# Third and fourth state-space tile begun at slots 9 and 14 instead of 8 and 12

## The chip, the cores and the metric

One core of a Trainium2 chip runs the whole layer in one launch. The metric is the device time of that launch in microseconds. The kernel before takes 855.93 us, the median of three runs (855.25 to 856.22).

## The reference, cut to what matters

One layer of a hybrid decoder on 512 tokens of width 1024, in float32. After an RMS norm, one projection gives the inputs of three branches and three gates; the branches are merged under the gates.

```
u, cb, cc, cx, q, k, v, gates = split_columns(rms_norm(x) @ w_in)
y_ssm  = s5_ssm(u, ...)            # 32 groups x 16 channels, 64 complex states per group
y_conv = short_conv(cb, cc, cx)
y_attn = swa_attention(q, k, v)
merged = sum_r sigmoid(gate_r) * (branch_r @ w_branch[r])
x += merged @ w_out;  x += SwiGLU(rms_norm(x));  x += sigmoid(rms_norm(x) @ w_pg) * (p @ w_pp)
```

Inside `s5_ssm` a diagonal complex recurrence runs over time; then `y = Re(C s) + D u`, a gelu, and a gate `y * sigmoid(y @ w_glu)`. Only the place of this state-space work in the program is touched here.

## The kernel before, in words

Every float32 product is made of three matmuls on parts (high and low of weights and of data). So the inner loop of a projection (`gemm_T`, lines 328 to 333) goes by groups of three 512-wide matmuls, and after each group `pump` (line 305) may add one piece of other work. A projection of 128 columns of `w_in` (`z_tile`, line 746) is eight groups; a pair of columns of `w_branch` (`branch`, line 1191) is two times four groups. Weights come by SyncE's DMA queue (`raw`, line 230), are cast to the high part on ScalarE (`hi`, line 245), and the low part is made on VectorE (`lo`, line 246). In this region a half of weights is cast three halves ahead of its use, and the slab after it is loaded when a slab's first half is cast.

The program order of each engine is written out by hand (the tile framework is in its manual mode). Three devices set it:

- `later(d, fn)` emits `fn` at the d-th group from now.
- `peq` holds TensorE work; `pump` emits one entry of it after a group.
- `slot()` (line 1175) is called after each eight groups; it moves every active state-space generator one stage on.

The state-space work is in four tiles of 128 channels (called tile 0 to tile 3), each a generator `ssm_gen` (line 1003), begun at the slot that `SSM_SLOTS` (line 1173) names. Its stages, one a slot:

- stage 0: loads of `tb` and `uu` (lines 1007, 1011).
- stage 1: `E` (1026 and 1028 on VectorE, `ewt` 1027 on GpSimd).
- stage 2: `W` (1067 to 1069) and the load of the tables `cs` (1071); TensorE gets `e_all`, the transposes of E (1039) and small products (1047). ScalarE copies them to `ET` (1040) and `ko` (1053), and SyncE spreads `ko` over `dbuf` (1057).
- stage 3: TensorE gets `v_two` (1083), which reads `ET`. In its own group it emits the first rotation and two groups on the second: `vsw` (1095, 1096 on ScalarE), `mt` and `G` (1092, 1098 on VectorE; `G` reads `cs`), three groups later subtraction, scan and `sv` (1102, 1104, 1111) with `gsw` (1107, 1108 on ScalarE, 1112 on GpSimd), and four groups later the addition 1114.
- stage 5: `Dg` (1123), two copies on ScalarE.
- stage 6: TensorE gets `y_one` (1130, 1132), which reads `Dg`, `sv` and `W`. Its result is copied to `ys` (1137), stored to `sy` (1140), `un` is loaded (1144).
- stage 7: load of `yr` (1150), behind the stores.
- stage 9: the gelu: `yc` (1155, VectorE), `qq` (1157, GpSimd), two VectorE operations two groups later (1163, 1164), the sigmoid on ScalarE four groups later (1167), `yu` (1168), and at seven groups its cast to `yh` on ScalarE (283).

Slots 0 to 4 lie beside the conv branch's merge, 5 to 12 beside the conv gates (each pair followed by two multiplications, 1211), 13 to 24 beside the attention gates and merge: two `z_tile` and one `branch` in turn (slots 15, 18, 21 and 24 come after a `branch`, whose two halves each emit 1200 and 1201 on VectorE). After slot 26 the program needs all four tiles. Each gate's result leaves PSUM by a sigmoid on ScalarE (1186), emitted just ahead of the slot.

Within one step the generators run in the order in which they began. Two lines of stage 9 and one of stage 5:

```
later(4, lambda: act.activation(out=qq, in_=qq, func=AF.Sigmoid, scale=1.5957691216057308))
later(7, lambda: split_ap(yu, ybox[0][0][:, ct], ybox[0][1][:, ct]))
act.copy(out=Dg[r, :, r].rearrange("p a (i q) -> p a i q", q=16), ...)
```

Of the kernel before, what the change touches and what calls it, by code (L numbers as in the profile page):

```python
# [77 lines left out]
def hybrid_trunk_kernel(  # L78
# [1091 lines left out]
        yield  # L1170

    slot_n = [0]
    SSM_SLOTS = {0: 0, 4: 1, 8: 2, 12: 3}

    def slot():
        if slot_n[0] in SSM_SLOTS:
            bg.append(ssm_gen(SSM_SLOTS[slot_n[0]]))
        slot_n[0] += 1
        step()
# [316 lines left out]
```

## Time and profile before

| what | value |
|---|---|
| median of three runs | 855.93 us |
| the profiled execution, its own time | 852.8 us |
| its span, first to last instruction | 851.0 us |
| TensorE busy | 98% of the span, mean granted clock 0.997 |
| VectorE, ScalarE, GpSimd busy | 66%, 45%, 15% |
| state-space tiles, lines 1007 to 1168 | from 175.1 to about 320 us |

The profile is one execution. A timeline's row is an instruction (or several alike, x4) with its start from the span's start, its duration, and in brackets the idle time of its engine before it with what ended it. Names such as `z<-h,hi` are the program's.

### The profile page before, as it was taken

The page shows a single profiled execution, that of the slowest core. Times are in us where ns is not written, and L with a number is a line of the kernel's source. Part 1 is how long each engine was busy: PE and PEld are TensorE (multiplying, and loading weights), DVE is VectorE, ACT ScalarE, POOL GpSimd, SP SyncE. Part 2 cuts the span into 40 slices and gives each one's busy share as a digit, 9 for nine tenths or more (in the row PEclk, how much of TensorE's full clock was granted, in tenths as well). Part 3 has the DMA queues.
Part 4 walks back from the last instruction along what each step waited for, and adds up shares of the span by engine and source line. Part 5 has one row for each costly group of instructions (what it writes and reads, how often), then busy time and mean ns, then how long its engine had stood idle before and what let it go on. Part 6 is the DMA issues. An engine that isn't in the chain of part 4 may idle for free.

```text
span 851.0 us, 10673 instructions
## 1 busy us (share of the span) xinstructions
PE 835.6 (98%) x4053; PEld 693.4 (81%) x4053; DVE 558.3 (66%) x833; ACT 382.9 (45%) x603; POOL 129.7 (15%) x135
## 2 busy tenths in 40 slices
PE   9999999999999999999999999999999999999996
PEld 7988777887877888888889888788888888888885
DVE  4889697848788863676885547644447444457964
ACT  6665657546444532443454333433333233334733
POOL 2040081724233311000003011000000000000201
PEclk9999999999999999999999999999999999999998
DMA  8759567553436359624858989962247422226112
GB/s 316 238 202 331 196 128 196 124 174 128 161 102 204 107 182 251 174 75 149 338 194 259 238 222 293 361 181 95 96 159 241 154 99 99 91 92 216 61 50 99
DMA packets 96035, 150.52 MB, mean 177 GB/s; under 512 B 6937, under 2 KB 67505, under 8 KB 93809
## 3 DMA queue, kind: packets, MB, share of 16 engines
q1 hardware_dynamic: 85056, 117.68, 40.6%
q0 software_dynamic: 10240, 31.46, 16.0%
q10 hardware_dynamic: 688, 0.70, 0.2%
q8 instruction: 32, 0.52, 0.2%
q14 instruction: 19, 0.15, 0.1%
HBM read 138.09 MB, written 43.00 MB: 213 GB/s over the span
## 4 chain that ended last, share of the span: by engine, by line
issue 38%; PE 32%; DVE 12%; DMA 8%; ACT 5%; POOL 5%; POOLq 0%; ACTq 0%; DVEq 0%
PE z L287 7%; PE z L288 7%; PE z L289 7%; DMA T<-T 4%; DMA T<-in_w_ffn_out_dram 2%; DVE lo L246 2%; PE z L1276 1%; PE z L1277 1%; PE z L1275 1%; PE z L1305 1%; PE z L1303 1%; PE z L1304 1%; PE z L683 1%; DVE s_t L853 1%; ACT s_t L867 1%
## 5 line engine op out<-in xcount | busy, mean ns | idle before, releaser
L287 PE MATMUL z<-h,hi 128*128 128x512 f32 (+1 forms) x776 | 293.6, 378 | 0.0
L288 PE MATMUL z<-l,hi 128*128 128x512 f32 (+1 forms) x776 | 290.5, 374 | 0.2 <-DVE l L284 0.2
L289 PE MATMUL z<-h,lo 128*128 128x512 f32 (+1 forms) x776 | 290.3, 374 | 0.0
L246 DVE TENSOR_TENSOR lo<-raw,hi 128x1024 fp32r<-128x1024 f32 (+1 forms) x168 | 206.3, 1232 | 108.4 <-ACT hi L245 107.9
L245 ACT CAST hi<-raw 128x1024 fp32r<-128x1024 f32 (+1 forms) x168 | 171.9, 1031 | 130.6 <-PE z L1305 37.7
L287 PEld LDWEIGHTS z<-h,hi 128*128 128x128 f32 x776 | 146.2, 188 | 26.1 <-issue 1.2
L289 PEld LDWEIGHTS z<-h,lo 128*128 128x128 f32 x776 | 146.1, 188 | 26.1
L288 PEld LDWEIGHTS z<-l,hi 128*128 128x128 f32 x776 | 146.2, 188 | 25.5 <-DVE l L284 0.7
L1303 PE MATMUL z<-hi,fh 128*128 128x512 f32 x180 | 70.8, 393 | 0.0
L1305 PE MATMUL z<-hi,fl 128*128 128x512 f32 x180 | 70.3, 390 | 0.0
L1304 PE MATMUL z<-lo,fh 128*128 128x512 f32 x180 | 70.1, 389 | 0.0
L1390 DVE TENSOR_TENSOR g<-z,g 128x512 f32<-128x512 f32 x22 | 15.2, 692 | 62.0 <-PE z L289 62.0
L1332 POOL TENSOR_SCALAR ms<-ss 128x1 f32<-128x1 f32 x8 | 3.0, 378 | 339.6 <-ACT xn L1329 339.5
L287 PE MATMUL z<-yh,hi 128*128 128x512 f32 x112 | 44.0, 393 | 0.0
L288 PE MATMUL z<-yl,hi 128*128 128x512 f32 x112 | 43.7, 390 | 0.2 <-DVE yl L284 0.2
L289 PE MATMUL z<-yh,lo 128*128 128x512 f32 x112 | 43.6, 390 | 0.0
L1305 PEld LDWEIGHTS z<-hi,fl 128*128 128x128 f32 x180 | 33.8, 188 | 7.5 <-DVE fl L284 0.5
L1304 PEld LDWEIGHTS z<-lo,fh 128*128 128x128 f32 x180 | 33.8, 188 | 6.8
L1303 PEld LDWEIGHTS z<-hi,fh 128*128 128x128 f32 x180 | 33.8, 188 | 6.7
L1382 ACT ACTIVATE g<-z 128x512 f32<-128x512 f32 x22 | 13.2, 598 | 55.2 <-PE z L289 55.2
L283 ACT CAST fh<-g 128x512 fp32r<-128x512 f32 (+1 forms) x22 | 11.2, 511 | 53.0 <-DVE g L1390 53.0
L1310 DVE TENSOR_TENSOR xr<-z,xr 128x512 f32<-128x512 f32 x36 | 24.5, 685 | 8.6 <-PE z L1305 7.9
(274 smaller groups left out, 1092.4 us busy)
## 6 DMA issues: line engine op xcount, KB each, us to landing
raw<-in_w_in_dram SPq DMA_DIRECT2D x23, 1024.0 KB, 5.3
raw<-in_w_ffn_in_dram SPq DMA_DIRECT2D x22, 1024.0 KB, 5.0
raw<-T SPq DMA_DIRECT2D x12, 1024.0 KB, 4.8
T<-in_w_ffn_out_dram POOLq DMA_DIRECT2D x12, 1024.0 KB, 12.0
T<-in_w_out_dram POOLq DMA_DIRECT2D x6, 1024.0 KB, 9.3
raw<-in_w_branch_dram SPq DMA_DIRECT2D x12, 512.0 KB, 3.9
raw<-in_w_ffn_out_dram SPq DMA_DIRECT2D x6, 1024.0 KB, 5.1
T<-in_w_ffn_out_dram POOLq DMA_DIRECT2D x6, 768.0 KB, 8.1
```

Source lines behind the costliest of these rows:

```text
L245: act.copy(out=hi, in_=src)
L246: todo = [lambda: dve.tensor_tensor(lo, src, hi.bitcast(F32), ALU.subtract)]
L283: act.copy(out=hi, in_=src)
L287: pe.matmul(ps, wh, ah, start=first, stop=False)
L288: pe.matmul(ps, wh, al, start=False, stop=False)
L289: pe.matmul(ps, wl, ah, start=False, stop=last)
L1303: pe.matmul(ps, fh[:, f, kk, ts], hi[:, k], start=st, stop=False, skip_group_check=True)
L1304: pe.matmul(ps, fh[:, f, kk, ts], lo[:, k], start=False, stop=False, skip_group_check=True)
L1305: pe.matmul(ps, fl[:, f, kk, ts], hi[:, k], start=False, stop=last, skip_group_check=True)
L1310: dve.tensor_tensor(dst, ps if sign > 0 else dst, dst if sign > 0 else ps, ALU.add if sign > 0 else ALU.subtract)
L1382: act.activation(out=g[:, i], in_=ps, func=AF.Silu)
L1390: dve.tensor_tensor(g[:, i], ps, g[:, i], ALU.mult)
```

## The change

```
-    SSM_SLOTS = {0: 0, 4: 1, 8: 2, 12: 3}
+    SSM_SLOTS = {0: 0, 4: 1, 9: 2, 14: 3}
```

Tile 2 begins one slot later, tile 3 two slots later; every stage of them moves by as much. No instruction is added or taken away. What moves against what, with the stages by slot:

| stage | tile 0 | tile 1 | tile 2 before, after | tile 3 before, after |
|---|---|---|---|---|
| 1 (E) | 1 | 5 | 9, 10 | 13, 15 |
| 2 (W, e_all, cs) | 2 | 6 | 10, 11 | 14, 16 |
| 3 (v_two) | 3 | 7 | 11, 12 | 15, 17 |
| 5 (Dg) | 5 | 9 | 13, 14 | 17, 19 |
| 6 (y_one) | 6 | 10 | 14, 15 | 18, 20 |
| 9 (gelu) | 9 | 13 | 17, 18 | 21, 23 |

## Rows read from the trace of the kernel before

**Rows 1.** The page, part 1: busy us and share of the span.

```profile
PE 835.6 (98%) x4053; PEld 693.4 (81%) x4053; DVE 558.3 (66%) x833; ACT 382.9 (45%) x603; POOL 129.7 (15%) x135
```

**Rows 2.** Waits of TensorE, 165 to 350 us: us in total, times, longest.

```profile
PE t L1083 <- ACT ET L1040: 1.2, 2, 0.6
...
PE t L1039 <- DVE E L1028: 0.7, 1, 0.7
```

**Rows 3.** Timeline of TensorE: start us, duration us, instruction, [idle before <- releaser].

```profile
239.35 0.50 PE L287 MATMUL z<-h,hi 128*128 128x512 f32 x1
...
247.28 1.34 PE L1083 MATMUL t<-uu,ET 64*128 64x128 f32 x16 [0.59 <-ACT ET L1040]
...
248.55 0.50 PE L287 MATMUL z<-h,hi 128*128 128x512 f32 x1
...
265.00 0.38 PE L1130 MATMUL t<-uu,Dg 128*128 128x128 f32 x2
```

**Rows 4.** Timeline of ScalarE gelu of tile 0, then Dg of tile 2.

```profile
234.27 0.83 ACT L1123 COPY Dg<-dbuf 64x256 f32<-64x256 f32 x2
...
242.09 0.63 ACT L1167 ACTIVATE qq<-qq 128x512 f32<-128x512 f32 x1 [5.91 <-DVE qq L1164]
...
245.22 1.04 ACT L245 CAST hi<-raw 128x1024 fp32r<-128x1024 f32 x1
...
246.16 0.59 ACT L1137 COPY ys<-t 128x512 f32<-128x512 f32 x1
...
249.41 0.58 ACT L1095 COPY vsw<-t 64x512 f32<-64x512 f32 x1
...
263.56 0.82 ACT L1123 COPY Dg<-dbuf 64x256 f32<-64x256 f32 x2
```

**Rows 5.** Timeline of VectorE: gelu of tile 0, then rotations of tiles 2 and 3.

```profile
236.27 0.74 DVE L1155 SCALAR_TENSOR_TENSOR yc<-un,vecs,yr 128x512 f32<-128x512 f32 x1
...
240.17 0.42 DVE L1163 TENSOR_SCALAR qq<-qq 128x512 f32<-128x512 f32 x1
...
240.62 1.43 DVE L1164 TENSOR_TENSOR qq<-qq,yc 128x512 f32<-128x512 f32 x1
...
250.62 0.69 DVE L1098 TENSOR_TENSOR G<-t,cs 128x512 f32<-128x512 f32 x1 [1.59 <-ACT vsw L1096]
...
280.06 0.68 DVE L1098 TENSOR_TENSOR G<-t,cs 128x512 f32<-128x512 f32 x1
...
290.32 0.68 DVE L1114 TENSOR_TENSOR sv<-sv,gsw 128x508 f32<-128x508 f32 x1
...
292.38 0.69 DVE L1114 TENSOR_TENSOR sv<-sv,gsw 128x508 f32<-128x508 f32 x1 [1.38 <-POOL gsw L1112]
```

**Rows 6.** Timeline of GpSimd, the gelu of tile 2.

```profile
294.94 1.04 POOL L1157 TENSOR_TENSOR qq<-yc 128x512 f32<-128x512 f32 x1 [2.60 <-DVE yc L1155]
```

**Rows 7.** Timeline of the SyncE queue: start us, issue time us.

```profile
179.27 1.05 SPq L230 DMA_DIRECT2D raw<-in_w_in_dram  x2
...
236.37 0.40 SPq L230 DMA_DIRECT2D raw<-in_w_branch_dram  x1
...
302.73 3.61 SPq L1140 DMA_DIRECT2D sy<-ys  x8
...
307.88 0.34 SPq L1150 DMA_DIRECT2D yr<-sy  x1
```

**Rows 8.** Line 1071, the load of cs: of tile 0, then of tile 2.

```profile
DMA to landing us min/median/max: 9.0/9.0/9.0
...
DMA to landing us min/median/max: 5.7/5.7/5.7
```

**Rows 9.** The page, part 6: KB each, median us to landing.

```profile
raw<-in_w_in_dram SPq DMA_DIRECT2D x23, 1024.0 KB, 5.3
```

**Rows 10.** End of the span: busy us by engine, PEclk, DMA share, GB/s.

```profile
843.00:845.00 2.00, 0.80 (x8) 0.65 (x6) 1.36 (x5) 1.04 (x4) 0.27 (x1) 1.00 0.35 132
...
846.00:851.00 5.00, 0.00 (x0) 0.00 (x0) 0.57 (x1) 0.59 (x1) 0.32 (x1) 0.50 0.27 105
```

## The prediction

> **What bounds the kernel now.** I read the page's part 1 first: TensorE is busy 98% of the span, so only what makes it wait counts [rows 1]. Then TensorE's waits in the stretch of the state-space tiles. The reader is to see two lines there: it waited twice for `ET` and once for `E`, 1.9 us together, all of it in tiles 2 and 3 [rows 2]. Then the timelines by engine. TensorE's shows the length of a slot: from 248.55, behind `v_two`, to `y_one` at 265.00 lie 24 groups, 0.685 us a group and 5.48 us a slot, and `y_one` found all its operands in time [rows 3]. ScalarE's timeline shows where `ET` lost its time. ScalarE stood idle for 5.91 us ahead of the gelu's sigmoid of tile 0 at 242.09, waiting for VectorE, while `y_one` of tile 1 had been done at 239.35; the copies of that result (`ys`, 246.16) and of `ET` came after the sigmoid, the cast of `yh` and a gate [rows 3, 4]. So what stands behind the sigmoid in ScalarE's program order pays for everything that the gelu waits for. `Dg` of tile 1 does not pay: it is emitted in the same step as the gelu but ahead of the delayed sigmoid, at 234.27 [rows 4].
>
> **What goes.** E of tiles 2 and 3 no longer shares its step with the gelu of the tile two before (slot 9 against 10, 13 against 15), so it is no longer behind that gelu's `qq` on GpSimd; and `e_all` no longer follows `y_one` in the same slot. `ET` of tile 2 is then copied behind `ys` (244.2, below), a gate and one cast, near 247, and wanted at 252.2. I count the labelled waits, -1.9 us [rows 2], and nothing more; the other end is 0, if both operands are late again.
>
> **What comes: Dg behind the sigmoid.** With spacings of five, the gelu of tile 1 is emitted at slot 13 and `Dg` of tile 2 at slot 14, that of tile 2 at 18 and `Dg` of tile 3 at 19. Four groups after the gelu's step comes its sigmoid, at seven groups `yh`, then a gate, then `Dg`. `Dg` now stands behind the sigmoid, and `y_one` reads it one slot later, still three slots behind `v_two` (17.7 us, 247.28 to 265.00 [rows 3]). No row of before has this order; so I add up the chain from `v_two` to `Dg`.
>
> From `v_two`'s start to the first `G`: about 1.1 us to its end, then 1.2 us as from `vsw` at 249.41 to `G` at 250.62 [rows 4, 5], 2.4 us with a free ScalarE. From `G` to the second addition 1114: 12.32 us (280.06 to 292.38, where it waited for GpSimd's `gsw`, in which wait the 0.74 us of `yc` fit) [rows 5]. `qq` is behind that `gsw` on GpSimd: 1.04 us [rows 6]; the first gelu operation takes 0.45 us to the second (240.17 to 240.62) [rows 5]. From the second to the place behind the next gate on ScalarE took 4.60 us (240.62 to 245.22 [rows 4, 5]); there a weight cast stood, now `Dg`, 0.83 us [rows 4]. Together G + 19.3 us, or `v_two` + 21.7 us, where 17.7 us are to be had: 4.0 us of wait at the least for tile 2.
>
> **What the loads add for tile 2.** SyncE's queue gets another order too. Its `tb` and `uu` pass nothing, but `cs` of tile 2 now stands behind `sy`, `un` and `yr` of tile 1, where it was issued ahead of them, and so does what follows `cs`: the weight slab that slot 12's group casts from, issued only one `z_tile` ahead of its use. `sy` waits for `ys`. With E gone from slot 9 the second gelu operation of tile 0 starts at 236.27 + 0.74 + 1.04 + 0.45 and small gaps, 238.65, so `ys` is copied 5.54 us later, as before (240.62 to 246.16), at 244.2 [rows 4 to 6]. `sy` from 244.8; `yr` waits for the stores to land, 5.15 us after the first (302.73 to 307.88), at 249.95; then `cs` at 250.4 and the slab at 250.9 [rows 7]. Landing of `cs`: 9.0 us behind the two 1 MB slabs at 179.27, 5.7 behind the half-size one at 236.37, so 2.2 us for each MB in front, and 4.6 to 5.7 us here: 255.0 to 256.1 [rows 7, 8]. The slab: 5.3 us [rows 9] plus 2.2 for `cs` in front less the 0.5 us of its head start, 257.9.
>
> TensorE's side: 239.35 to 247.28 are eight groups, `e_all` and 0.6 us of wait; with one slot more and no wait `v_two` begins at 252.2 and `y_one` is reached at 269.9 [rows 3]. The cast of the slab stands ahead of `vsw` on ScalarE: 257.9 to 258.9, `vsw`, and `G` at 260.05 instead of 254.6. `Dg` is done at 260.05 + 19.3 = 279.4. The wait of tile 2: 9.5 us. Its ends are 4.0 us (no load late) and 11.5 us (the slab in 9.0 us); I take 9.5.
>
> **Tile 3.** After that wait ScalarE is level with TensorE, so `sy` and `cs` follow `y_one` at once and `cs` has a slot and more in hand. But its `v_two` lies in a `branch`: four more VectorE operations (1200, 1201, twice) of some 0.68 us, overlapped to 2.6, get between the rotations and the gelu, and fill the wait for `gsw`, so `yc` counts. 2.4 + 10.26 (`G` to the first addition, 280.06 to 290.32) + 0.6 + 2.6 + 0.74 + 1.04 + 0.1 + 0.45 + 4.6 - 0.74 (the second gelu operation at 0.69 us, as its like in these rows, without GpSimd beside it) + 0.83 = 22.9 us against 17.7: 5.2 us. Ends: 2.6 us, if those four fall into waits, and 7.8, if something as long comes between.
>
> **The clock.** [...] Bounds: nothing, or one slot at half, 5.48 us, for each wait. I take 1 us each, 2.0 us, since `y_one` itself, the next work, is short.
>
> [...]
>
> **Sum.** -1.9 + 9.5 + 5.2 + 2.0 = +14.8 us. On the profiled execution's own 852.8 us that is 867.6; the median of the runs, 855.93, lies 3.1 us above it, and on it I get 870.7.
>
> **Rivals.**
> - The loads are in time. The slab's data may come with the same packets as `cs`, before ScalarE needs it. Then `G` waits for `cs` at 255.5 at most, `Dg` is done at 274.8, the wait is 4.9 us: +10.2, 866.1 (with no load late 865.2). For it: the bare 5.3 us of a slab [rows 9]. Against: `ys` lags `y_one` by five us even so.
> - Only one of the two waits comes, because VectorE's operations overlap better than summed: -1.9 + 4.0 + 1.0 = +3.1, 859.0.
> - The clock falls in both waits and stays low for a slot behind each: +12.8 + 11.0, 879.7. For it: the 0.50 within 2 us of the last work [rows 10]. Against: `y_one` comes first, and a slot at half is only my bound. [...]
> - Faster: `Dg` is in place before `y_one` and only the relief is left. The point is the 17.7 us between `v_two` and `y_one`: if the chain of rotations, gelu and `Dg` fits in, nothing comes, and -1.9 us make 854.0. For it: in before `Dg` of tile 2, begun at 263.56, was done 0.6 us ahead of `y_one` [rows 3, 4]. Against: there the sigmoid and `yh` stood behind `Dg`, now they stand ahead of it.
> - No change: a wait for `Dg` of about 1.9 us in all eats the relief, 855.9.
>
> **Chances.** Forecast 0.50, loads in time 0.20, one wait 0.11, low clock 0.10, faster 0.05, no change 0.04. About 0.2%, 1.7 us, is what a measurement of this kernel can tell from nothing. So faster 0.05, within 0.04, slower 0.91. The range goes from the one-wait case to the low-clock case, 859 to 880 us, and takes in the bounds of the loads.
>
> **What would show it.** Right: TensorE waits at line 1130 for ScalarE's `Dg` (1123) twice, some 9.5 and 5.2 us, and no more at 1039 and 1083; on ScalarE the sigmoid 1167 waits for VectorE ahead of each; a weight cast waits for its DMA near 252 to 258; the granted clock falls below 1.00 in the first wait. Wrong: no wait at 1130, or one under 2 us, or a wait of TensorE for `sv` or weights instead.

## The result and the profile after

The changed kernel takes 879.51 us (median of four runs, 878.28 to 881.02), the kernel before beside it 855.59: ratio 1.0282, 95% interval 1.0268 to 1.0296, or +23.9 us. The forecast was +14.8 us.

The page first: part 1's share of TensorE, then its row and the granted clock's in part 2, 40 slices of 22 us. The reader is to see TensorE idle in slices 13 (263 to 285 us) and 15 (307 to 329 us), and a granted clock (PEclk, in tenths of full speed) below full in slices 13, 14 and 16.

```profile
PE 845.6 (96%) x4053; PEld 700.2 (80%) x4053; DVE 563.3 (64%) x833; ACT 383.4 (44%) x603; POOL 130.9 (15%) x135
...
PE   9999999999994979999999999999999999999996
...
PEclk9999999999997898999999999999999999999998
```

TensorE's waits from 165 to 350 us (in total, times, longest). The lines for `ET` and `E` are gone; one line is new: 17.6 us for `Dg` in place of 1.9 us [rows 2]. (Both kernels have one more, of 0.2 us for `yl`.)

```profile
PE t L1130 <- ACT Dg L1123: 17.6, 2, 11.3
```

TensorE's timeline, as [rows 3]. From `v_two` of tile 2 at 255.37 to the last matmul ahead of `y_one`, 272.69, it is 17.3 us, against 17.5 in the kernel before (247.28 to 264.77); then TensorE stands idle for 11.29 us. `y_one` itself, 284.37 to 289.78, takes 5.4 us, where that of tile 1 took 3.0 in the kernel before (236.31 to 239.35); the matmuls behind it follow each other at 0.43 us, where it was 0.23 ahead of the wait, and only from 292.47 at 0.23 again. Tile 3 repeats it from 320.82.

```profile
255.37 1.16 PE L1083 MATMUL t<-uu,ET 64*128 64x128 f32 x16
...
272.69 0.39 PE L289 MATMUL z<-h,lo 128*128 128x512 f32 x1
...
284.37 0.80 PE L1130 MATMUL t<-uu,Dg 128*128 128x128 f32 x2 [11.29 <-ACT Dg L1123]
...
289.78 0.80 PE L287 MATMUL z<-h,hi 128*128 128x512 f32 x1
...
290.37 0.63 PE L288 MATMUL z<-l,hi 128*128 128x512 f32 x1
...
290.80 0.63 PE L289 MATMUL z<-h,lo 128*128 128x512 f32 x1
...
292.47 0.39 PE L287 MATMUL z<-h,hi 128*128 128x512 f32 x1
...
303.50 0.71 PE L1083 MATMUL t<-uu,ET 64*128 64x128 f32 x8
...
320.82 0.39 PE L289 MATMUL z<-yh,lo 128*128 128x512 f32 x1
...
327.53 0.80 PE L1130 MATMUL t<-uu,Dg 128*128 128x128 f32 x2 [6.32 <-ACT Dg L1123]
```

ScalarE's timeline says why, as [rows 4]. `Dg` at 283.50 stands behind the sigmoid of tile 1's gelu (280.38, which waited 3.77 us for VectorE), the cast of `yh` and a gate. And the whole rotation began late: the weight cast at 261.79 had waited 6.39 us for its DMA, with `vsw` behind it, though `v_two` was done near 256.5. At 326.66 `Dg` of tile 3 stands in the same order, with no late weights.

```profile
261.79 1.05 ACT L245 CAST hi<-raw 128x1024 fp32r<-128x1024 f32 x1 [6.39 <-DMA raw<-in_w_in_dram]
...
262.86 0.58 ACT L1095 COPY vsw<-t 64x512 f32<-64x512 f32 x1
...
280.38 0.63 ACT L1167 ACTIVATE qq<-qq 128x512 f32<-128x512 f32 x1 [3.77 <-DVE qq L1164]
...
282.49 0.62 ACT L283 CAST yh<-yu 128x512 fp32r<-128x512 f32 x1 [1.48 <-DVE yu L1168]
...
283.01 0.59 ACT L1186 ACTIVATE sg<-z 128x512 f32<-128x512 f32 x1
...
283.50 0.82 ACT L1123 COPY Dg<-dbuf 64x256 f32<-64x256 f32 x2
...
326.66 0.82 ACT L1123 COPY Dg<-dbuf 64x256 f32<-64x256 f32 x2
```

VectorE's timeline, as [rows 5]: from the first `G` at 264.07 to the second addition it is 12.8 us, and the gelu stands behind it.

```profile
264.07 0.69 DVE L1098 TENSOR_TENSOR G<-t,cs 128x512 f32<-128x512 f32 x1 [7.34 <-ACT vsw L1096]
...
276.91 1.51 DVE L1114 TENSOR_TENSOR sv<-sv,gsw 128x508 f32<-128x508 f32 x1 [1.16 <-POOL gsw L1112]
...
278.35 1.27 DVE L1163 TENSOR_SCALAR qq<-qq 128x512 f32<-128x512 f32 x1
...
279.65 0.69 DVE L1164 TENSOR_TENSOR qq<-qq,yc 128x512 f32<-128x512 f32 x1
```

SyncE's queue, as [rows 7]: it issues the stores of `ys` from 248.37, `yr` after they had landed, then the tables, then the weight slab at 254.42, 7.4 us ahead of the cast.

```profile
248.37 3.58 SPq L1140 DMA_DIRECT2D sy<-ys  x8
...
253.56 0.34 SPq L1150 DMA_DIRECT2D yr<-sy  x1
...
253.95 0.42 SPq L1071 DMA_DIRECT2D cs<-tb  x1
...
254.42 0.43 SPq L230 DMA_DIRECT2D raw<-in_w_in_dram  x1
```

Last the clock. A row is a stretch of time, its length, the busy us of each engine, then the granted clock, the DMA share and GB/s. The first row is dealt with at the end of the document. In the first wait the clock is at 0.50, and stays there in the work behind it, until the matmuls are 0.23 us apart again at 292.47: 8 us of work. It falls again for some 9 us of work behind the second wait.

```profile
33.00:43.00 10.00, 10.00 (x70) 9.50 (x69) 8.34 (x41) 5.63 (x9) 0.00 (x0) 0.83 0.59 190
...
276.00:284.30 8.30, 0.00 (x0) 0.00 (x0) 6.20 (x6) 3.02 (x6) 3.34 (x3) 0.50 0.16 48
...
284.30:292.00 7.70, 7.63 (x29) 5.03 (x30) 6.41 (x9) 2.69 (x4) 1.22 (x1) 0.50 0.49 159
...
297.00:317.00 20.00, 20.00 (x105) 16.49 (x104) 12.72 (x16) 6.80 (x14) 4.83 (x3) 1.00 0.42 144
...
327.50:336.50 9.00, 8.97 (x32) 6.04 (x33) 2.45 (x2) 3.06 (x4) 0.00 (x0) 0.50 0.41 132
```

In the kernel before the clock was full in all of this region:

```profile
165.00:350.00 185.00, 182.81 (x909) 147.47 (x908) 131.01 (x159) 82.96 (x134) 51.78 (x43) 1.00 0.56 168
```

The profiled execution is 3.5 us behind that of before already at `v_two` of tile 1 (222.27 against 218.76), ahead of everything that moved. So the change is worth 877.8 - 851.0 - 3.5 = 23.3 us there.

### The profile page after: what moved, and what is told of

It is laid out like the page before. It is cut to its first block, busy times and chain, and to the rows that moved or that the text cites. A ratio compares the mean times of both kernels' runs of the same rounds, so it can differ in the third digit from the quotient of the medians.

```text
span 877.8 us, 10665 instructions
## 1 busy us (share of the span) xinstructions
PE 845.6 (96%) x4053; PEld 700.2 (80%) x4053; DVE 563.3 (64%) x833; ACT 383.4 (44%) x603; POOL 130.9 (15%) x135
## 4 chain that ended last, share of the span: by engine, by line
issue 36%; PE 35%; DVE 11%; DMA 8%; ACT 5%; POOL 4%; SPq 0%; POOLq 0%; DVEq 0%; ACTq 0%
PE z L287 7%; PE z L288 7%; PE z L289 7%; DMA T<-T 4%; DMA T<-in_w_ffn_out_dram 2%; DVE lo L246 2%; PE z L1276 1%; PE z L1277 1%; PE z L1275 1%; PE z L1305 1%; PE z L1303 1%; PE z L1304 1%; PE z L683 1%; DVE s_t L853 1%; ACT s_t L867 1%
## 5 line engine op out<-in xcount | busy, mean ns | idle before, releaser
L1332 POOL TENSOR_SCALAR ms<-ss 128x1 f32<-128x1 f32 x8 | 3.0, 376 | 333.1 <-ACT xn L1329 332.9
L283 ACT CAST fh<-g 128x512 fp32r<-128x512 f32 (+1 forms) x22 | 11.2, 511 | 53.0 <-DVE g L1390 53.0
L1186 ACT ACTIVATE sg<-z 128x512 f32<-128x512 f32 x24 | 14.3, 596 | 44.5 <-PE z L289 44.3
```

Of the source, the lines that this page charges most:

```text
L283: act.copy(out=hi, in_=src)
L1186: act.activation(out=sg, in_=ps, func=AF.Sigmoid)
```

## The experiments

Each is compared with runs of the kernel before that were taken beside it on the same chip. Theory A says that `Dg` behind the sigmoid on ScalarE makes TensorE wait, that a late weight slab lengthens the first wait, and that the clock falls in the waits. Each expectation names its rival.

### The order of Dg alone, forward and backward

`e1_dg_early`: the changed kernel, `Dg` of tiles 2 and 3 one stage earlier; `dg` is the two copies of stage 5 as a function.

```
         peq.append(lambda: [v_two(a) for a in range(4)])
         yield
+        if ct >= 2:
+            dg()
         yield
+        if ct < 2:
+            dg()
         yield
```

> The changed kernel with the copies to Dg of tiles 2 and 3 emitted one slot earlier (in the step of the gelu, ahead of the delayed sigmoid), all else as in it. Theory A (Dg behind the sigmoid on ScalarE makes TensorE wait): no wait of TensorE for Dg is left; what can be late instead is the second addition of tile 2's rotation, which in the changed kernel's trace ended at 278.4 against 272.9, when y_one was reached, so one wait at y_one of about 5 us for VectorE in tile 2 and under 0.5 us in tile 3, with part of the clock's cost: 859 to 864 us. Theory B (the late weight slab is what costs, and Dg only shows it): the two waits stay as long and are put down to another engine: 877 to 881 us.

861.32 us against 855.12, ratio 1.0064 (1.0041 to 1.0087): the time is as theory A had it. Its waits (line 1137 is `y_one` on `Dg` here, 1139 on `sv`):

```profile
PE t L1137 <- ACT Dg L1123: 3.7, 1, 3.7
...
PE t L1139 <- DVE sv L1114: 0.6, 1, 0.6
```

The wait of tile 3 is gone, that of tile 2 is down from 11.3 to 4.3 us. One thing is not as expected: most of the rest is put down to `Dg` still, not to VectorE. `Dg` no longer stands behind the sigmoid, but behind `gsw` of its own rotation, and that is late by the slab: the weight cast ahead of it waited 6.70 us for its DMA here too.

`e7_before_dg_late`: the kernel before, slots 8 and 12, with `Dg` of tiles 2 and 3 put behind the sigmoid.

```
         yield
+        if ct >= 2:
+            later(8, dg)
+        else:
+            dg()
```

> The kernel before (slots 8 and 12) with the copies to Dg of tiles 2 and 3 emitted eight groups later, behind the sigmoid and yh of the tile before, the rest as in it: the order of the changed kernel without its slots. Theory A: TensorE waits for Dg in both tiles, 9 to 11 us in tile 2 and 6 to 8 us in tile 3 (the sigmoid's place in the trace of before, 271.4 and 297.2, plus 3 to 4 us, against y_one at 265.0 and 294.4), the clock falls behind both: 874 to 884 us. Rival (the slots and the loads make the loss, the order of Dg is harmless): within 2 us of 855.6.

878.05 us against 854.66, ratio 1.0269 (1.0253 to 1.0285). Not one slot is changed, and nearly the whole loss is there:

```profile
PE t L1137 <- ACT Dg L1123: 16.5, 2, 9.8
...
PE t L1083 <- ACT ET L1040: 0.6, 1, 0.6
```

So the order of two small copies on ScalarE is enough for a loss of this size. That the two totals agree so well is partly chance. In `e7` the gelu's step stands one slot ahead of `y_one`, in the changed kernel two: in the trace of before the sigmoid begins at 271.43, 6.4 us after TensorE reached `y_one` at 265.00, and in `e7`, with the slots and loads of before, where no cast ahead of `vsw` waits for its slab, the longer wait is 9.8 us. In the changed kernel the same order alone is worth less, 5.7 us in tile 2, and the late slab makes up the rest (`e3` below). One wait for `ET` is still there, as expected of the old slots.

### One tile at a time

`e4_only_tile2` and `e5_only_tile3` change the slots alone:

```
-    SSM_SLOTS = {0: 0, 4: 1, 8: 2, 12: 3}
+    SSM_SLOTS = {0: 0, 4: 1, 9: 2, 13: 3}     # e4
+    SSM_SLOTS = {0: 0, 4: 1, 8: 2, 13: 3}     # e5
```

> Slots 9 and 13: tile 2 moved, tile 3 four slots behind it as before, so that its Dg is emitted in the step of tile 2's gelu again, ahead of the sigmoid. Theory A: one wait for Dg, in tile 2, of 11 us, with the clock's cost behind it of 3.5 to 4; none in tile 3, where E and ET may be late again by some 1.3 us: 868 to 871 us. Rival (any later start of the tiles costs, by slots): about half of the loss, 867, but with waits in both tiles.

868.81 us against 855.12, ratio 1.0150 (1.0127 to 1.0172).

```profile
PE t L1130 <- ACT Dg L1123: 11.2, 1, 11.2
```

> Slots 8 and 13: tile 3 alone moved, by one slot, so that its Dg comes a step behind tile 2's gelu while tile 2 is as in the kernel before. Theory A: no wait for Dg in tile 2 (E and ET of tile 2 late by 0.6 us as before), one in tile 3 of 4 to 11 us with 3 to 4 us of clock behind it (its place among gates and branches is another, so its size is open): 862 to 870 us. Rival (only tile 2's move hurts, by its loads): 855 us.

863.40 us against 854.66, ratio 1.0100 (1.0080 to 1.0120).

```profile
PE t L1130 <- ACT Dg L1123: 7.1, 1, 7.1
...
PE t L1083 <- ACT ET L1040: 0.6, 1, 0.6
```

A tile waits where it stands five slots behind the one before, and not where it stands four behind, even in slot 13 of `e4`, which is later than the old 12. The rival "later is worse" would have put waits into both. In `e5` tile 2 keeps its old 0.6 us for `ET`.

### The late slab

`e3_stores_late`: the changed kernel, with the stores of tile 1 behind the tables and the slab in SyncE's queue; `store` is the eight stores and the load of `un`, and the load of `yr` comes one slot later.

```
+            if ct == 1:
+                later(9, store)
+            else:
+                store()
...
+        if ct == 1:
+            yield
         yr = sp_.tile(SC, F32, tag="yb", name="yr", bufs=1)
```

> The changed kernel with the stores of tile 1's result (sy, un) emitted nine groups later and its load of yr one slot later, so that the tables of tile 2 and the weight slab pass them on SyncE's queue. Theory A (the first wait is made of 4 us of bare chain and some 6 to 7 us of a late weight slab, on which the cast ahead of the rotation's copies waits): the cast's wait falls from 6.4 us to about 1, tile 2's wait for Dg from 11.3 to 5 to 6 us, tile 3's stays at 6.3: 872 to 875 us. Rival (the slab's delay lies beside the chain): both waits stay, 879 us.

872.20 us against 855.12, ratio 1.0192 (1.0170 to 1.0214). Waits of TensorE, two in all, of which 6.3 us is the longest and so 5.7 the other:

```profile
PE t L1130 <- ACT Dg L1123: 12.0, 2, 6.3
```

The longer is tile 3's 6.3 us of the changed kernel again, so the shorter one, 5.7 us, is put down to tile 2. And the cast that waited 6.39 us for its DMA, on ScalarE's timeline:

```profile
253.55 1.05 ACT L245 CAST hi<-raw 128x1024 fp32r<-128x1024 f32 x1 [0.70 <-DMA raw<-in_w_in_dram]
```

The slab made 5.6 us of the first wait (11.3 to 5.7); what is left is the bare chain of rotation, gelu and `Dg`.

### The clock

`e2_fill` and `e10_fill_more` are the changed kernel with work for TensorE put into the waits. The result stays the same, since the added products are overwritten.

```
         def y_one(a):
+            if a == 0:
+                for _ in range({2: 40, 3: 22}.get(ct, 0)):       # e10: 50 and 28
+                    pe.matmul(yps, hTh[:, 0, 0:128], hTh[:, 0], start=True, stop=True)
```

> The changed kernel with work for TensorE in the place of the two waits: 40 matmuls of 128x512 ahead of y_one of tile 2 and 22 ahead of that of tile 3 (9.1 and 5.0 us at the full clock; their results are overwritten by y_one). They end inside the waits of 11.3 and 6.3 us. Theory A (the clock falls because TensorE stands idle and costs some 7.8 us behind the waits): the waits shrink to about 2 and 1.3 us, the granted clock stays at 1.00 from 270 to 340 us, and the time falls by 6 to 8 us to 871.5 to 873.5 us. Rival (work behind the waits is slow for another reason, such as late weights): the time stays at 879 to 880 us.

876.40 us against 855.12, ratio 1.0238 (1.0211 to 1.0266): of the 6 to 8 us only 3 to 4 came. The waits shrank to 2.1 and 1.3 us as expected, but the clock fell after all, in `y_one` behind those short waits:

```profile
284.50:292.00 7.50, 7.19 (x35) 5.02 (x36) 5.96 (x8) 2.94 (x4) 0.78 (x1) 0.77 0.53 174
...
325.00:335.00 10.00, 9.00 (x36) 6.35 (x37) 3.60 (x4) 3.98 (x7) 0.00 (x0) 0.66 0.41 128
```

So this one missed, and did not settle the rival. In `e10_fill_more` the fill was made as long as the waits:

> The changed kernel with 50 and 28 matmuls of 128x512 ahead of y_one of tiles 2 and 3 in place of 40 and 22 (11.3 and 6.4 us at the full clock, as long as the waits themselves). Theory A (half the time behind the waits is the clock's: 7.9 and 9.0 us at half, some 8 us): no wait over 0.5 us, the clock at 1.00 from 270 to 340 us, 871 to 873.5 us. Rival (the clock falls in y_one itself, whatever came ahead of it): it falls behind 282 and 322 us all the same and the time is 876 us or more.

871.36 us against 855.05, ratio 1.0198 (1.0180 to 1.0216), 0.0084 below the changed kernel's ratio, 7.2 us (the two were not measured side by side). No wait at `y_one` over 0.3 us is left, and the clock stays:

```profile
270.00:290.00 20.00, 19.71 (x98) 15.34 (x97) 16.20 (x21) 8.45 (x13) 5.54 (x4) 1.00 0.26 84
...
315.00:340.00 25.00, 25.00 (x121) 19.72 (x120) 13.86 (x17) 8.29 (x13) 1.91 (x2) 1.00 0.36 116
```

With these products in the place of the 17.6 us of waiting, the mean clock was 1.00 from 165 to 350 us too, where the changed kernel has 0.93. So 7 to 8 us of the loss are the clock's. By the trace of the changed kernel it is about as much: some 8.0 us (284.37 to 292.4) and 9.3 us (327.53 to 336.8) of work at 0.50, half of which, with matmuls 0.43 us apart in place of 0.23, is 8.6 us as an estimate.

### Other slots, and a repair

`e6_spacing6`: six slots between tiles.

```
+    SSM_SLOTS = {0: 0, 4: 1, 10: 2, 16: 3}
```

> Slots 10 and 16: two steps apart between the gelu of one tile and Dg of the next, and the gelu's step falls ahead of the rotations' group, so the sigmoid waits only for the first of them. Theory A: Dg still stands behind the sigmoid in ScalarE's order but the sigmoid is early, so no wait for Dg; E and ET of tiles 2 and 3 are in time too: the relief alone, 852.5 to 854 us, faster than the kernel before by 1.5 to 3. Rival (the further the tiles move the worse, because their end comes near the end of the region): at least one wait at y_one or, behind slot 26, for the last tile, 857 us or more.

856.20 us against 854.66, ratio 1.0013 (1.0000 to 1.0026): no loss to speak of, but not the gain that was expected either. Two waits are left:

```profile
PE t L1130 <- ACT Dg L1123: 2.5, 2, 1.4
```

ScalarE's timeline shows tile 2's: the weight cast waits for the slab here too (4.70 us), so that `gsw` at 275.01 is late, and `yh` of the gelu, a gate and a cast come between it and `Dg`.

```profile
257.91 1.05 ACT L245 CAST hi<-raw 128x1024 fp32r<-128x1024 f32 x1 [4.70 <-DMA raw<-in_w_in_dram]
...
275.01 0.62 ACT L1107 COPY gsw<-R 64x512 f32<-64x512 f32 x1 [3.37 <-DVE sv L1110]
...
276.29 0.62 ACT L283 CAST yh<-yu 128x512 fp32r<-128x512 f32 x1
...
278.24 0.83 ACT L1123 COPY Dg<-dbuf 64x256 f32<-64x256 f32 x2
```

`e9_before_gelu_late` and `e8_after_gelu_late` leave `Dg` and move the gelu: its sigmoid, `yu` and `yh` come behind the next step instead, at 10, 11 and 12 groups, and two buffers more make room.

```
-        later(4, lambda: act.activation(out=qq, in_=qq, func=AF.Sigmoid, scale=1.5957691216057308))
+        later(10, lambda: act.activation(out=qq, in_=qq, func=AF.Sigmoid, scale=1.5957691216057308))
...
-        later(7, lambda: split_ap(yu, ybox[0][0][:, ct], ybox[0][1][:, ct]))
+        later(12, lambda: split_ap(yu, ybox[0][0][:, ct], ybox[0][1][:, ct]))
```

> The kernel before (slots 8 and 12) with the same later sigmoid, yu and yh. Theory A: ET is no longer behind the sigmoid, so its two waits of 0.6 us go; E stays behind the gelu's qq on GpSimd and may be late by up to 0.7 us in tile 3: 853 to 855 us. Rival (ET was late for another reason): as the kernel before, both waits of 0.6 us kept.

854.09 us against 855.05, ratio 0.9989 (0.9978 to 1.0000). Both waits for `ET` are gone, and the one for `E` is 1.1 us in place of 0.7:

```profile
PE t L1039 <- DVE E L1028: 1.1, 1, 1.1
```

> The changed kernel (slots 9 and 14) with the gelu's sigmoid, yu and yh emitted 10, 11 and 12 groups behind the gelu's step in place of 4, 5 and 7 (two more buffers so that the next tile's ys has a place), for all tiles: Dg and ys now stand ahead of the sigmoid on ScalarE. Theory A: both waits go, and so does the late slab, since ys of tile 1 is copied at once; no wait of TensorE from 170 to 350 us, the relief of 2 to 2.5 us alone: 852.5 to 854 us, faster than the kernel before by 1 to 2.5. Rival (something else of the new slots is late at y_one, such as the rotation's additions): a wait at y_one of 1 us or more, 856 us or above.

858.89 us against 855.05, ratio 1.0044 (1.0028 to 1.0060): the rival's number. One wait of 2.8 us for `Dg` is left, in tile 2, and again it is the slab, for which the cast ahead of `vsw` waited 4.34 us, held in SyncE's queue by another wait: `yr` of tile 1 needs the buffer that tile 0's `yl`, now later, still reads.

```profile
SPq L1150 <- DVE yl L284: 2.3, 1, 2.3
```

`e11_dg_early_stores_late` joins `e1` and `e3`, its edits are theirs.

> The changed kernel with both single repairs: Dg of tiles 2 and 3 one slot earlier, and tile 1's stores behind the weight slab. Theory A (the two causes are the order of Dg and the late slab): what was left of the wait in tile 2 with Dg alone moved, 4.3 us, goes with the slab's lateness; waits at y_one of 0 to 0.5 us, clock at 1.00: 853 to 855 us. Rival (the stores' delay was worth only what Dg's order was worth): a wait of 2 us or more stays in tile 2, 857 us or above.

856.91 us against 855.05, ratio 1.0024 (1.0012 to 1.0036), 2 us above what was expected. The waits for `Dg` are gone, as expected; a new one of 2.3 us is there, for `E` of tile 3, which was not. In VectorE's program order it stands behind tile 1's gelu and the products of the branch.

```profile
PE t L1039 <- DVE E L1028: 2.3, 1, 2.3
```

`e12_gelu_late_yr_late` is `e8` with tile 1's `yr` one slot later (the second edit of `e3`).

> As the changed kernel with the later sigmoid (e8), and tile 1's load of yr one slot later, since in e8 that load waited on SyncE's queue for yl of tile 0 (2.3 us) and held the tables and the weight slab behind it, so that the cast ahead of the rotation waited 4.3 us and TensorE 2.8 us for Dg. Theory A: the slab is issued some 3 us earlier, the cast waits 1 us or less, no wait of TensorE from 170 to 350 us and the clock stays: 852.5 to 854.5 us, at or below the kernel before. Rival (Dg behind two gates and a cast is too late whatever the slab does): the wait of 2 us or more at y_one stays, 857 us or above.

854.82 us against 855.61, ratio 0.9993 (0.9981 to 1.0004), 0.3 us above the expected range. The cast waits for no DMA, and TensorE's waits for the tiles are 1.0 us in all:

```profile
PE t L1130 <- ACT Dg L1123: 0.5, 1, 0.5
...
PE t L1039 <- DVE E L1028: 0.5, 1, 0.5
```

So with slots 9 and 14 the whole loss of 24 us is undone by the order on two queues. No version beats both kernels beyond its interval; `e9`, whose interval ends at 1.0000, is the nearest.

## Why the prediction was right

The mechanism, the place and the sign came as forecast; +14.8 us had been summed, 23.9 came. The time, 879.51 us, lies within the range only by 0.5 us, and the upper end of 880 was set by the low-clock rival, which had a chance of 0.10; that the range held is in part luck. Term by term:

- **Relief, -1.9 us.** The waits for `E` and `ET` are gone, as forecast. That this is worth 1.9 us no run shows by itself: in `e9` and `e12` TensorE waits 1.1 and 1.0 us in place of 1.9, and they are 1.0 and 0.8 us below the kernel before, with intervals that reach it.
- **Tile 2, forecast 9.5 us, measured 11.3.** `v_two` to `y_one` is as forecast. The slab, forecast to leave SyncE 1.3 us ahead of `v_two`, left it 0.95 ahead and took 7.4 us until the cast, 7.0 forecast. The chain from `G` to the end of `Dg` was put at 19.3 us and is 20.3 (264.07 to 284.32): the second addition and the first gelu operation ran beside GpSimd (`qq` and `ewt`, 276.84 to 279.34), 1.51 and 1.27 us in place of 0.69 and 0.42 [rows 5]. `e3` splits the wait: the slab's share was forecast at 5.5 us (9.5 - 4.0) and is 5.6, the bare chain's at 4.0 and is 5.7, so the miss is the chain's. `e1` shows the share of the order.
- **Tile 3, forecast 5.2 us, measured 6.3.** From `v_two` at 303.50 to the end of `Dg` at 327.48 it is 24.0 us, 22.9 forecast; more of VectorE's work ran beside GpSimd: beside `gsw` (313.24 to 315.08 and 318.31 to 319.61) the subtraction 1102 took 1.78 us and the addition 1201 1.25, where without it they took 0.68 and 0.69 (309.94, 313.23).
- **The clock, forecast 2.0 us, measured 7 to 8.** This is the term that was mis-sized, and makes more than half of the 9 us that were missing. The bound, a slot at half for each wait (11 us in both), was right; the value was not. No run shows a cost of 1 us behind a wait, which was the author's estimate: the runs showed 0.50 for 8.0 and 9.3 us of work behind the two waits, and 7.2 us less time where `e10` keeps the clock at 1.00. "`y_one` itself, the next work, is short" was the reason given, and it was the wrong way round: `y_one` at 0.50 takes 5.4 us instead of 3, done at 289.8 and 332.9, and the clock came back only at 292.4 and 336.8. A row of the end of the span [rows 10], where nothing runs behind, was all that the estimate had to go by.

-1.9 + 17.6 + 8 = 23.7 us, against 23.9 measured and 23.3 in the profile. Of the rivals, "loads in time" is refuted by the cast's 6.39 us, "one wait" by the two waits, "faster" and "no change" by the result. The low-clock case (879.7) gave the number, and of the clock it had the mechanism better than the forecast: the clock fell in both waits and stayed low for 8 and 9 us of work behind them. But it cost less than that case assumed (7 to 8 us, not 11.0), and the waits were longer than it assumed (17.6 us, not 14.7), so part of the agreement is two errors that cancel.

## What to carry to other kernels

Before work is moved by a slot, list on each queue what it comes to stand behind, DMA queues and small copies included. On ScalarE the two copies of `Dg`, 0.82 us long, stood behind a sigmoid that had waited 3.77 us for VectorE, and in `e7` that order alone made the kernel 2.7% slower. On SyncE's queue the slab stood behind the stores of `ys` and the load of `yr`, and the cast waited 6.39 us for it; with the stores behind it, in `e3`, 0.70 us.

A wait of TensorE is to be priced with the work behind it, not only with its own length. Behind the waits of 11.3 and 6.3 us the clock was 0.50 for 8.0 and 9.3 us of work; behind the 2.8 us of `e8` matmuls were 0.43 us apart from 278.86 to 281.84; and in `e1`, `e3`, `e4` and `e7`, whose longest waits are 3.7 to 11.2 us, the mean clock from 165 to 350 us was 0.92 to 0.97, against 1.00 in the kernel before. Of the shorter waits some had such work behind them, those of `e2` (2.1 and 1.3 us, clock 0.77 and 0.66).

## What the runs showed that was not expected

The clock also falls where TensorE is busy by the profile. From 33 to 43 us of the changed kernel's trace it is busy for all of 10.00 us and the clock is 0.83; in the trace of before it was 1.00 in the same stretch:

```profile
33.00:43.00 10.00, 10.00 (x85) 9.96 (x86) 8.66 (x44) 7.86 (x12) 0.00 (x0) 1.00 0.59 202
```

Of the other kernels' traces `e1`, `e4`, `e10`, `e11` and `e12` have 0.83 there, `e2` 0.66, `e3` and `e7` 1.00, though nothing there was changed. In the changed kernel's trace it falls behind a run of sixteen small transposes (line 469, 34.02 to 35.95): the four of line 481, at 36.34, take 0.98 us, 0.60 in before. In `e2_fill` the clock fell in `y_one`, small matmuls too, behind waits of only 2.1 and 1.3 us, while `e6_spacing6` kept it behind 1.4 and 1.1 and `e11_dg_early_stores_late` behind 2.3 (1.00 in both from 165 to 350 us). What decides between these was not tried. The dip alone does not make the scatter of 3 to 4 us among runs of one kernel. The changed kernel's trace is 1.0 us behind that of before ahead of the dip (the transposes begin at 34.02 and 33.06 us) and 2.5 us behind it (the first 512-wide matmul of `z`, at 45.87 and 43.37), so it cost 1.5 of the 3.5 us; another 1.0 came near 99 us, at a wait for `s_t` that before does not have. What makes the rest of the scatter is open.
